# Left-hand sums of a joint feed-forward stage: built in PSUM beside the LayerNorm's transposes, with other banks and lanes around them

## The chip, the cores and the metric

The kernel runs on one core of a Trainium2 chip, in one launch. The metric is device time in microseconds. A core has TensorE (PE, matrix products into PSUM, with PEld for its weight loads), VectorE (DVE), ScalarE (ACT), GpSimd (POOL) and SyncE (SP), which here issues loads. PSUM has 8 banks of 128 partitions x 512 float32.

## The reference, cut to what matters

One decoder layer in float32, 1024 positions, width 1024. The change lies in its second part and just ahead of it.

```
mix = hybrid_mixer(x, ...)          # convolution group, attention group, output projection w_out
x   = layer_norm(ALPHA * x + mix, ln1_g, ln1_b)
h   = causal_depthwise_conv(x @ w_up, dw_w, dw_b)      # w_up: 1024 x 5632, conv width 3
g, u = jnp.split(h, 2, axis=-1)
ffn = (jax.nn.silu(g) * u) @ w_down                    # w_down: 2816 x 1024
x   = layer_norm(ALPHA * x + ffn, ln2_g, ln2_b)
```

In the mixer's convolution group a depthwise convolution of width 31 is followed by a LayerNorm over channels and a swish (`conv_norm` in the kernel).

## The kernel before, in words

**Precision.** Each float32 operand is split into a high part (a cast on ACT, L232, L280, L749) and a low part (the rest, by a subtraction). A product is three: high x high, high x low, low x high. So `mm3` (L266, L267, L269) issues 24 matmuls for 1024 inputs and `product` (L790, L791, L793) 12 for 512 inputs. Weights are split the same way into lanes `wh` (ACT) and `wl` (POOL, L234).

**Halves.** Positions are worked on in two halves of 512, H = 0 and 1, of four row blocks (t) each. After the mixer each half goes through the first LayerNorm (`ln1`), whose blocks are transposed on PE (L277), copied and split from PSUM (L280, L281) into `x1T[H]`: high and low parts of the channels' two halves, [128, 4, 512] each.

**Feed-forward.** D_FF is cut into 22 chunks of 128. The first six ("alone") are computed for each half separately: `up` (two `up_branch` products of 24 matmuls, convolution of width 3, silu, gate; L673 to L694) for two chunks, then `down` (L713 to L715, added to `acc` by L720). The other 16 ("joint") are computed for both halves at once with seven products instead of eight block products (a Strassen scheme): `joint_up` takes products of sums of weight blocks (`tsum`, L829, on POOL, lanes `ts`) with left-hand sides in `left`, some of which are sums of blocks of `x1T`. `left_sums` builds sums 1, 3 and 2 for k = 0 to 3 by DVE additions in SBUF lanes `u` (L743 for the first, L745 for further terms), and `keep` splits each into sums' areas (L749 on ACT, L750 on POOL). `last_sum` builds sum 4 the same way, just before `joint`. A chunk's products go in the order 1, 6, 7, 2, 5, 4, 3; the sums are used by products 6 (sum 2), 7 (sum 3), 5 (sum 1) and 3 (sum 4).

**Order.** `SCRIPT` is a string of letters, each of which takes one step of a generator: A attention of the second half, C its convolution, N its conv norm, o and O the output projections of the two halves, l and L the two first LayerNorms (four row blocks each), f the alone chunks of the first half (up, up, down, three times: f1 to f9), s the left-hand sums (four steps). What is left is drained at the end, then come `last_sum`, `joint`, and the second half's alone chunks. This is the order of emission. A planner in the build then places the instructions of each engine by its own model of costs and due times; the result is a fixed queue for each engine, with semaphores. Three kinds of work keep the emitted order: loads on SP (`load`), the large products on PE (`chain`), and the convolution's taps.

**PSUM.** `PT` names for each user a string of bank families, used in turn; `PS` says how many banks each family has: A 2, S 2, T 1, Y 1, C 2. The attention uses S for scores, T for transposes and Y for its output; the convolution and conv norm use C; the output projections A.

**SBUF.** Lanes are numbered pieces of 2 KB per partition. Tiles of one tag go through its lanes in turn, so a lane's next user waits for the last one's readers. `area(i)` is lanes 4i to 4i + 3 and `pair(i)` areas 2i and 2i + 1. The residual rows `acc` of the second half lie in lanes 64 to 71, loaded at the start of `second_out`; `pair(5)` is lanes 40 to 47, which hold the first half's attention output, later the gates of the first alone group (`gh`, `gl`), later sum 1. The rows g1 and b1 of the LayerNorm lie in lanes 94 to 97, where the lanes `u` also lie.

Of the kernel before, what the change touches and what calls it, by code (L numbers as in the profile page):

```python
# [10 lines left out]
F32 = mybir.dt.float32  # L11
F32R = mybir.dt.float32r
AF = mybir.ActivationFunctionType
ALU = mybir.AluOpType
# [20 lines left out]
GROUP = 2  # L35
ALONE = 6
SCRIPT = ('0hx00j0hxixxiiiacaaaaaaaaaaaaannnaaagaggqqgaaaqkqoAAAoAAAAAo'
          'ACAoAAllAANAAAANAlAlfNfAOOOfOffLLLLsffffsss')
SKEW = (1, 2, 5)
KOFF = (4, 5)  # L40
AHEAD = 1
# [1 line left out]
XM = (1, 1)  # L43
PT = {'x0': 'AT', 'x1': 'AS', 'glu0': 'AS', 'glu1': 'A', 'kv0': 'A', 'kv1': 'A', 'q0': 'A', 'q1': 'A', 'v0': 'T', 'v1': 'T',
      'joint': 'ATSACSYC',
      'tail': 'T', 'out0': 'A', 'out1': 'A', 'ln0': 'A', 'ln1': 'A', 'up0': 'AY', 'up1': 'AY', 'down0': 'SCY', 'down1': 'S'}
PS = {'A': 2, 'S': 2, 'T': 1, 'Y': 1, 'C': 2}
UNIT = 512
BASE = 384
# [7 lines left out]
    'oh': [16, 17, 18, 19, 20, 21], 'ol': [22, 23, 24, 25, 26, 27], 'or': [28, 30],  # L57
    'gh': [40, 41, 42, 43], 'gl': [44, 45, 46, 47],
}
LANES_NORM1 = {'nsum': [68, 69], 'nz': [70], 'nsq': [64, 65, 66, 67]}  # L60
LANES_OUT1 = {'bo': [32], 'oh': [48, 49, 50, 51, 52], 'ol': [53, 54, 55, 38, 39], 'or': [34, 36]}
LANES_FFN = {'gh': [D0 + i for i in range(28, 32)], 'gl': [D0 + i for i in range(24, 28)]}
LANES_JOINT = {'z': [D0 + i for i in (17, 18, 19, 36)],
               'ts': [D0 + i for i in (32, 33, 34)], 'u': [D0 + i for i in (20, 21, 22, 23)],
               'wl': [D0 + i for i in (12, 13, 14, 15, 16, 35)]}
FREE = [i for a in (0, 1, 2, 3, 5) for i in range(8 * a, 8 * a + 8)]
LANES_END = {'g2': [D0 + 32], 'b2': [D0 + 34], 'wl': [D0 + i for i in range(12, 17)], 'gh': FREE[0:6], 'gl': FREE[6:12], 'dh': FREE[12:24], 'dl': FREE[24:36]}

# [2 lines left out]
def hybrid_layer_kernel(  # L71
# [35 lines left out]
    def psk(key, shape=(P, 512)):  # L107
        tags = PT[key]
        k = ps_turn[key] = ps_turn.get(key, -1) + 1
        return psB(shape, tags[k % len(tags)])  # L110

    def f(ap):
        return ap.bitcast(F32)
# [156 lines left out]
        chain(m[0], m[-1])  # L270

    def transpose_split(src, xh, xl, t, key):
        for q in range(2):
            b = psk(key)
            for k in range(4):
                kt = q * 4 + k
                nc.tensor.transpose(out=b[:, k * P:(k + 1) * P], in_=src[:, kt * P:(kt + 1) * P], identity=ident)  # L277
            bv_ = b.rearrange("p (k t) -> p k t", t=P)
            hd = xh[q][:, :, t * P:(t + 1) * P]
            nc.scalar.copy(out=hd, in_=bv_)  # L280
            nc.vector.tensor_tensor(out=xl[q][:, :, t * P:(t + 1) * P], in0=bv_, in1=f(hd), op=ALU.subtract)  # L281

    def bcast_row(v, tag):
        t = sbt([P, D], tag)
# [39 lines left out]
    def pair(i):  # L324
        return area(2 * i), area(2 * i + 1)
# [330 lines left out]
    def ln1(H, g, b):  # L656
        (h0, l0), (h1, l1) = [pair(i) for i in ((2, 3) if H == 0 else (4, 6))]
        xh, xl = (h0, h1), (l0, l1)
        x1T[H] = (xh, xl)
        for t in range(TB):  # L660
            a = acc[H * TB + t]
            layer_norm_rows(a, g, b, H)
            transpose_split(a, xh, xl, t, "ln%d" % H)
            nc.scalar.mul(out=a, in_=a, mul=ALPHA)
            yield

    def up_branch(H, u):
# [68 lines left out]
    left = {}  # L736
    turns = [0]

    sums = {n: [[a[:, k, :] for k in range(4)] for a in pair(i)] for n, i in ((1, 5), (3, 0), (2, 1), (4, 2))}

    def add(o, *terms):
        (x0, s0), (x1, s1) = terms[0], terms[1]
        nc.vector.tensor_tensor(out=o, in0=x0, in1=x1, op=ALU.add if s1 > 0 else ALU.subtract)  # L743
        for x_, s_ in terms[2:]:
            nc.vector.tensor_tensor(out=o, in0=o, in1=x_, op=ALU.add if s_ > 0 else ALU.subtract)  # L745

    def keep(n, k, o):
        h, l = [x_[k] for x_ in sums[n]]
        nc.scalar.copy(out=h, in_=o)  # L749
        nc.gpsimd.tensor_tensor(out=l, in0=o, in1=f(h), op=ALU.subtract)  # L750

    def left_sums():
        a1h, a1l = x1T[1]
        a2h, a2l = x1T[0]

        o = {}
        for k in range(4):
            p1h, p1l, p2h, p2l = [[f(a[i][:, k, :]) for i in range(2)] for a in (a1h, a1l, a2h, a2l)]
            for n in (1, 3, 2):
                o[n] = sbt([P, HALF], "u")  # L760
                if n == 1:
                    add(o[n], (p2h[0], 1), (p2h[1], 1), (p2l[0], 1), (p2l[1], 1))
                elif n == 3:
                    add(o[n], (p1h[0], 1), (p2h[0], -1), (p1l[0], 1), (p2l[0], -1))
                else:
                    add(o[n], (o[1], 1), (p1h[0], -1), (p1l[0], -1))
                keep(n, k, o[n])
            yield

    def last_sum():  # L770
        a1h, a1l = x1T[1]
        a2h, a2l = x1T[0]
        for k in range(4):
            o = sbt([P, HALF], "u")
            s2h, s2l = [f(x_[k]) for x_ in sums[2]]
            add(o, (f(a1h[1][:, k, :]), 1), (s2h, -1), (f(a1l[1][:, k, :]), 1), (s2l, -1))
            keep(4, k, o)

        def ks(a):
            return [a[:, k, :] for k in range(4)]  # L780

        left.update({1: (ks(a1h[0]), ks(a1l[0])), 2: (ks(a1h[1]), ks(a1l[1])), 3: sums[4], 4: (ks(a2h[1]), ks(a2l[1])),
                     5: sums[1], 6: sums[2], 7: sums[3]})
# [211 lines left out]
    def second_norm():  # L995
# [4 lines left out]
             'c': conv(0), 'a': attn(0), 'n': conv_norm(0), 'g': glus(1), 'k': once(lambda: proj_kv(1)),  # L1000
             'q': proj_q(1), 'A': attn(1), 'o': out_proj(0), 'l': first_norm(), 'C': conv(1),
             'N': second_conv_norm(), 'f': ffn(0, alone), 'O': second_out(), 'L': second_norm(),
             's': left_sums()}
    drain(load_x(0))
    parameters()
    for k in SCRIPT:
# [64 lines left out]
```

## Time and profile before

| | |
|---|---|
| median of three runs | 1154.1 us (1151.25 to 1156.5) |
| the profiled execution's own time | 1154.67 us |
| its span, first to last instruction | 1152.9 us |
| mean granted TensorE clock | 0.958 |
| busy: PE, DVE, ACT, POOL | 1085.0, 796.6, 521.8, 627.5 us |
| second half's output projection | about 400 to 457 us |
| second half's LayerNorm, alone chunks f4 to f9, sums | about 450 to 559 us |
| joint stage, nothing else beside it | from about 563 us |

How to read it: a row of a group gives line, engine, operation, output tile <- input tiles, shapes, how many (x), then busy time in us and the mean ns of one, then the engine's idle time ahead of it and what ended it. A row of waits says who waited for whom: us in total, how often, the longest. A row of one source line gives the ns of the shortest, the median and the longest, and the first and last start. In the chain of waits a row gives start, length, engine, tile and line. The strip PEclk gives the granted clock in tenths over 40 equal slices. `psA`, `psT` and so on are banks of the families above; `x` is any area, `cy` the lanes that `u` shares with the convolution's outputs, `bo` the lanes of b1.

### The profile page before, as it was taken

The numbers are of one execution on the slowest core, as the hardware profiler recorded it, in microseconds if no ns is written. First come the engines' busy times: TensorE is split into PE (matmuls) and PEld (weight loads), VectorE is DVE, ScalarE is ACT, GpSimd is POOL, SyncE is SP. The second block draws the span as 40 slices with busy tenths as digits, with TensorE's granted clock in tenths as the row PEclk, the third lists the DMA queues.
The fourth block names the chain that finished last, engine by engine and source line by source line (L and its number), as shares of the span: only waits on it lengthen the run. The fifth ranks groups of instructions, "written<-read, shape, count | busy, mean of one in ns | idle before, by whom it ended". The sixth has DMA issues, their size and how long they took to land.

```text
span 1152.9 us, 14636 instructions
## 1 busy us (share of the span) xinstructions
PE 1085.0 (94%) x5257; PEld 907.7 (79%) x5257; DVE 796.6 (69%) x1406; ACT 521.8 (45%) x1031; POOL 627.5 (54%) x484
## 2 busy tenths in 40 slices
PE   7999999998898999894999999999999999999997
PEld 5877788888787799683778787887878787888875
DVE  2699556999994436889784747465665656559666
ACT  4536897673678322453342425152424242442530
POOL 4739644365451255867856556463637373735561
PEclk9999988999977899997999999999999999999999
DMA  5544213124101333221121212121202021133421
GB/s 177 165 100 120 74 26 98 52 85 144 38 1 54 102 99 94 76 71 37 37 73 37 74 37 74 37 65 32 69 19 89 22 73 37 56 109 110 128 92 73
DMA packets 115643, 85.21 MB, mean 74 GB/s; under 512 B 20355, under 2 KB 108018, under 8 KB 115570
## 3 DMA queue, kind: packets, MB, share of 16 engines
q1 hardware_dynamic: 112368, 78.92, 23.1%
q10 hardware_dynamic: 3201, 5.35, 1.3%
q8 instruction: 41, 0.67, 0.2%
q14 instruction: 33, 0.26, 0.1%
HBM read 80.05 MB, written 4.21 MB: 73 GB/s over the span
## 4 chain that ended last, share of the span: by engine, by line
PE 71%; DVE 18%; DMA 4%; ACT 4%; POOL 1%; issue 1%; SPq 0%; POOLq 0%; DVEq 0%; ACTq 0%
PE psA L266 4%; PE psA L267 4%; PE psA L269 4%; DVE psC L423 4%; DVE cy L745 3%; PE psC L793 2%; PE psS L509 2%; PE psC L790 2%; PE psC L791 2%; PE psS L713 2%; PE psS L714 2%; PE psS L715 2%; PE psS L790 2%; PE psS L791 2%; PE psS L793 2%; PE psA L790 2%
## 5 line engine op out<-in xcount | busy, mean ns | idle before, releaser
L234 POOL TENSOR_TENSOR wl<-raw,wh 128x512 fp32r<-128x512 f32 x196 | 267.3, 1375 | 187.4 <-ACT wh L232 80.8
L232 ACT CAST wh<-raw 128x512 fp32r<-128x512 f32 x196 | 118.9, 618 | 169.2 <-PE psA L267 26.8
L234 POOL TENSOR_TENSOR wl<-ts,wh 128x512 fp32r<-128x512 f32 x64 | 83.0, 1304 | 148.3 <-ACT wh L232 136.0
L423 DVE SCALAR_TENSOR_TENSOR psC<-hconv,const,psC 128x512 f32<-128x512 f32 x196 | 135.9, 745 | 0.0
L266 PE MATMUL psA<-x,wh 128*128 128x512 f32 x288 | 115.8, 402 | 3.1 <-ACT wh L232 2.0
L232 ACT CAST wh<-ts 128x512 fp32r<-128x512 f32 x64 | 39.4, 622 | 173.3 <-PE psC L715 31.0
L267 PE MATMUL psA<-x,wh 128*128 128x512 f32 x288 | 115.7, 402 | 0.0
L269 PE MATMUL psA<-x,wl 128*128 128x512 f32 x288 | 76.4, 400 | 0.0
L266 PEld LDWEIGHTS psA<-x,wh 128*128 128x128 f32 x288 | 55.2, 192 | 15.7 <-ACT wh L232 2.3
L267 PEld LDWEIGHTS psA<-x,wh 128*128 128x128 f32 x288 | 55.4, 192 | 11.9 <-issue 0.7
L269 PEld LDWEIGHTS psA<-x,wl 128*128 128x128 f32 x288 | 54.1, 191 | 12.7 <-issue 1.0
L291 POOL TENSOR_TENSOR tiny<-tiny,const 128x1 f32<-128x1 f32 (+1 forms) x28 | 26.5, 950 | 68.0 <-DVE tiny L290 68.0
L234 POOL TENSOR_TENSOR ol<-or,oh 128x512 fp32r<-128x512 f32 x32 | 40.5, 1292 | 32.5 <-ACT oh L232 32.5
L720 DVE TENSOR_TENSOR acc<-psS,acc 128x512 f32<-128x512 f32 x48 | 32.9, 687 | 24.5 <-PE psS L715 24.4
L790 PE MATMUL psS<-x,wh 128*128 128x512 f32 x112 | 43.7, 390 | 0.8 <-ACT wh L232 0.8
L790 PE MATMUL psA<-x,wh 128*128 128x512 f32 x112 | 44.2, 395 | 0.0
L791 PE MATMUL psA<-x,wh 128*128 128x512 f32 x112 | 44.0, 393 | 0.0
L791 PE MATMUL psS<-x,wh 128*128 128x512 f32 x112 | 43.6, 389 | 0.0
L790 PE MATMUL psC<-x,wh 128*128 128x512 f32 x112 | 43.6, 389 | 0.0
L791 PE MATMUL psC<-x,wh 128*128 128x512 f32 x112 | 43.6, 389 | 0.0
L413 POOL TENSOR_TENSOR cp<-cp,cp 128x512 f32<-128x512 f32 x28 | 36.1, 1289 | 13.3 <-ACT cp L409 13.3
L713 PE MATMUL psC<-wh,gh 128*128 128x512 f32 x80 | 32.5, 407 | 11.3 <-ACT gh L693 8.7
(331 smaller groups left out, 3237.5 us busy)
## 6 DMA issues: line engine op xcount, KB each, us to landing
raw<-in_w_up SPq DMA_DIRECT2D x56, 512.0 KB
raw<-in_w_down SPq DMA_DIRECT2D x28, 512.0 KB
raw<-in_w_in SPq DMA_DIRECT2D x20, 512.0 KB
raw<-in_x SPq DMA_DIRECT2D x8, 512.0 KB
raw<-in_w_in SPq DMA_DIRECT2D x16, 256.0 KB
acc<-in_x SPq DMA_DIRECT2D x8, 512.0 KB
or<-in_w_out SPq DMA_DIRECT2D x64, 64.0 KB
or<-in_w_out SPq DMA_DIRECT2D x8, 512.0 KB
```

The costliest lines, as they stand in the source:

```text
L232: nc.scalar.copy(out=h, in_=part)
L234: nc.gpsimd.tensor_tensor(out=l, in0=part, in1=f(h), op=ALU.subtract)
L266: m.append(nc.tensor.matmul(out=o, lhsT=wh[kt], rhs=xh[kt], start=kt == 0, stop=False))
L267: m.append(nc.tensor.matmul(out=o, lhsT=wh[kt], rhs=xl[kt], start=False, stop=False))
L269: m.append(nc.tensor.matmul(out=o, lhsT=wl[kt], rhs=xh[kt], start=False, stop=kt == KT - 1))
L413: nc.gpsimd.tensor_tensor(out=extra[c], in0=extra[c], in1=prod, op=ALU.add)
L423: tap(nc.vector.scalar_tensor_tensor(out=to, in0=src, scalar=cdw(k, c), in1=chains[c], op0=ALU.mult, op1=ALU.add))
L713: m.append(nc.tensor.matmul(out=o, lhsT=gh[:, tsl], rhs=wh, start=j == 0, stop=False))
L745: nc.vector.tensor_tensor(out=o, in0=o, in1=x_, op=ALU.add if s_ > 0 else ALU.subtract)
L790: m.append(nc.tensor.matmul(out=o, lhsT=wh[k], rhs=xh[k], start=k == 0, stop=False))
L791: m.append(nc.tensor.matmul(out=o, lhsT=wh[k], rhs=xl[k], start=False, stop=False))
L793: m.append(nc.tensor.matmul(out=o, lhsT=wl[k], rhs=xh[k], start=False, stop=k == 3))
```

## The change

- Left-hand sums. The first sum (of the first half's blocks only) becomes a generator of its own, `first_sums`: three additions in a PSUM bank of family T per k, then the split, its low part on DVE. Sums 3 and 2 and the unsplit sum 4 are built by `other_sums`, called in `ln1` for each row block of the second half: it goes on working in the two banks that the block's transposes filled (`transpose_split` now returns them), with the low parts on DVE as well. Sum 4 is parked in `last_f` (lanes 106 to 109, which `ts` uses later), and `last_sum` only splits it.
- Order: the four s steps move from the end to around the last O step, ahead of f4, f5 and the L steps.
- Banks: the second LayerNorm's transposes go from A to T and C in turn; the first half's alone chunks from A and Y to A (up) and from S, C and Y to S and Y (down); the first sums take T.
- Lanes: the second conv norm (`second_conv_norm`) takes its temporaries from lanes 40 and 42 to 47 instead of 64 to 70. The sixth `wl` lane is added in `last_sum` rather than at the first L step.

```
-SCRIPT = (...
-          'ACAoAAllAANAAAANAlAlfNfAOOOfOffLLLLsffffsss')
+          'ACAoAAllAANAAAANAlAlfNfAOOOfsOsssffLLLLffff')
-      ..., 'ln1': 'A', 'up0': 'AY', 'up1': 'AY', 'down0': 'SCY', 'down1': 'S'}
+      ..., 'ln1': 'TC', 'sum1': 'T', 'up0': 'A', 'up1': 'AY', 'down0': 'SY', 'down1': 'S'}
-LANES_NORM1 = {'nsum': [68, 69], 'nz': [70], 'nsq': [64, 65, 66, 67]}
+LANES_NORM1 = {'nsum': [44, 45], 'nz': [40], 'nsq': [42, 43, 46, 47]}
...
-            transpose_split(a, xh, xl, t, "ln%d" % H)
+            banks = transpose_split(a, xh, xl, t, "ln%d" % H)
             nc.scalar.mul(out=a, in_=a, mul=ALPHA)
+            if H == 1:
+                other_sums(t, *[b.rearrange("p (k t) -> p k t", t=P) for b in banks])
...
+    last_f = at((D0 + 32) * 4 * UNIT, [P, 4, HALF], F32, "lastf")
+    def part(x_, t):
+        return x_[:, :, t * P:(t + 1) * P]
+    def into(o, x0, x1, op):
+        nc.vector.tensor_tensor(out=o, in0=x0, in1=x1, op=op)
+    def split_to(h, l, o):
         nc.scalar.copy(out=h, in_=o)
-        nc.gpsimd.tensor_tensor(out=l, in0=o, in1=f(h), op=ALU.subtract)
+        into(l, o, f(h), ALU.subtract)
+    def first_sums():
+        (h0, h1), (l0, l1) = x1T[0]
+        for k in range(4):
+            o = psk("sum1")
+            into(o, f(h0[:, k, :]), f(h1[:, k, :]), ALU.add)
+            into(o, o, f(l0[:, k, :]), ALU.add)
+            into(o, o, f(l1[:, k, :]), ALU.add)
+            split_to(*[x_[k] for x_ in sums[1]], o)
+            yield
+    def other_sums(t, b0, b1):
+        (h0, h1), (l0, l1) = [[f(part(a, t)) for a in x_] for x_ in x1T[0]]
+        into(b0, b0, h0, ALU.subtract)
+        into(b0, b0, l0, ALU.subtract)
+        split_to(*[part(a, t) for a in pair(area_of[3])], b0)
+        into(b0, h1, b0, ALU.subtract)
+        into(b0, b0, l1, ALU.add)
+        s2h, s2l = [part(a, t) for a in pair(area_of[2])]
+        split_to(s2h, s2l, b0)
+        into(b1, b1, f(s2h), ALU.subtract)
+        into(part(last_f, t), b1, f(s2l), ALU.subtract)
     def last_sum():
...
-            add(o, (f(a1h[1][:, k, :]), 1), (s2h, -1), (f(a1l[1][:, k, :]), 1), (s2l, -1))
-            keep(4, k, o)
+            split_to(*[x_[k] for x_ in sums[4]], last_f[:, k, :])
+        lanes['wl'] = [D0 + i for i in (12, 13, 14, 15, 16, 35)]
```

More of the change, by code (lines that the diff above doesn't have):

```diff
@@ L45 @@
       'joint': 'ATSACSYC',
-      'tail': 'T', 'out0': 'A', 'out1': 'A', 'ln0': 'A', 'ln1': 'A', 'up0': 'AY', 'up1': 'AY', 'down0': 'SCY', 'down1': 'S'}
+      'tail': 'T', 'out0': 'A', 'out1': 'A', 'ln0': 'A', 'ln1': 'TC', 'sum1': 'T', 'up0': 'A', 'up1': 'AY', 'down0': 'SY', 'down1': 'S'}
 PS = {'A': 2, 'S': 2, 'T': 1, 'Y': 1, 'C': 2}
@@ L63 @@
 LANES_JOINT = {'z': [D0 + i for i in (17, 18, 19, 36)],
-               'ts': [D0 + i for i in (32, 33, 34)], 'u': [D0 + i for i in (20, 21, 22, 23)],
-               'wl': [D0 + i for i in (12, 13, 14, 15, 16, 35)]}
+               'ts': [D0 + i for i in (32, 33, 34)], 'u': [D0 + i for i in (20, 21, 22, 23)]}
 FREE = [i for a in (0, 1, 2, 3, 5) for i in range(8 * a, 8 * a + 8)]
@@ L272, in transpose_split @@
     def transpose_split(src, xh, xl, t, key):
+        banks = []
         for q in range(2):
             b = psk(key)
+            banks.append(b)
             for k in range(4):
@@ L281, in transpose_split @@
             nc.vector.tensor_tensor(out=xl[q][:, :, t * P:(t + 1) * P], in0=bv_, in1=f(hd), op=ALU.subtract)
+        return banks
     def bcast_row(v, tag):
@@ L737, in hybrid_layer_kernel @@
     turns = [0]
[L739 to L756, printed above, removed]
-        for k in range(4):
[L758 to L767, printed above, removed]
-            yield
+    area_of = {1: 5, 3: 0, 2: 1, 4: 2}
@@ new lines, in hybrid_layer_kernel @@
+    sums = {n: [[a[:, k, :] for k in range(4)] for a in pair(i)] for n, i in area_of.items()}
+    last_f = at((D0 + 32) * 4 * UNIT, [P, 4, HALF], F32, "lastf")
[4 more added lines that the diff above has]
+    def split_to(h, l, o):
+        nc.scalar.copy(out=h, in_=o)
+        into(l, o, f(h), ALU.subtract)
+    def first_sums():
+        (h0, h1), (l0, l1) = x1T[0]
+        for k in range(4):
+            o = psk("sum1")
[3 more added lines that the diff above has]
+            split_to(*[x_[k] for x_ in sums[1]], o)
+            yield
@@ L773, in last_sum @@
         for k in range(4):
-            o = sbt([P, HALF], "u")
-            s2h, s2l = [f(x_[k]) for x_ in sums[2]]
-            add(o, (f(a1h[1][:, k, :]), 1), (s2h, -1), (f(a1l[1][:, k, :]), 1), (s2l, -1))
-            keep(4, k, o)
+            split_to(*[x_[k] for x_ in sums[4]], last_f[:, k, :])
+        lanes['wl'] = [D0 + i for i in (12, 13, 14, 15, 16, 35)]
         def ks(a):
@@ L1002, in hybrid_layer_kernel @@
              'N': second_conv_norm(), 'f': ffn(0, alone), 'O': second_out(), 'L': second_norm(),
-             's': left_sums()}
+             's': first_sums()}
     drain(load_x(0))
```

## The prediction

> **What bounds the kernel now.** I read the page's head first, then the strips over the span, then the table of stretches, cut where the stages change.
>
> ```profile
> PE 1085.0 (94%) x5257; PEld 907.7 (79%) x5257; DVE 796.6 (69%) x1406; ACT 521.8 (45%) x1031; POOL 627.5 (54%) x484
> PEclk9999988999977899997999999999999999999999
> 347.00:400.00 53.00, 44.97 (x210) 40.21 (x209) 23.54 (x51) 31.65 (x65) 12.76 (x12) 0.77 0.27 84
> 400.00:457.00 57.00, 57.00 (x433) 55.03 (x432) 28.54 (x56) 13.72 (x23) 28.83 (x23) 1.00 0.33 98
> 457.00:480.00 23.00, 22.25 (x100) 18.04 (x98) 20.36 (x26) 7.68 (x12) 19.85 (x11) 1.00 0.23 69
> 480.00:501.00 21.00, 16.66 (x76) 13.37 (x76) 16.38 (x26) 12.12 (x21) 8.89 (x7) 0.84 0.17 50
> 501.00:523.00 22.00, 22.00 (x98) 18.02 (x96) 21.93 (x22) 9.49 (x16) 19.54 (x12) 1.00 0.28 83
> 523.00:563.00 40.00, 24.13 (x84) 18.65 (x84) 38.81 (x45) 13.34 (x23) 31.77 (x21) 0.79 0.07 21
> 563.00:1060.00 497.00, 488.77 (x2148) 402.43 (x2147) 313.02 (x524) 185.17 (x312) 270.00 (x211) 1.00 0.19 59
> ```
>
> In a stretch's row stand its length, the busy time of PE, PEld, DVE, ACT and POOL, then the granted clock. PE is busy for 488.77 of 497 us from 563 on, at full clock, and for all of 400 to 457: there only less PE work would help, and the change removes none. The loss lies in two places. From 457 to 563 PE is busy for 22.25 + 16.66 + 22.00 + 24.13 = 85.0 of 106 us, and the clock falls to 0.84 and 0.79. From 347 to 400 it idles for 8.0 us at a clock of 0.77.
>
> What ends last in 457 to 563 is said by the chain of waits there and by the waits of PE:
>
> ```profile
> 554.61 1.20 DVE cy L745 x2
> 555.81 1.20 DVE acc L720 x2
> 557.01 0.79 DVE cy L745
> 557.83 0.62 ACT x L749
> 558.45 0.53 ACT wh L232
> 559.02 0.50 PE psS L790
> 562.49 0.91 PE psS L793 x4
> PE psC L713 <- ACT gh L693: 8.7, 1, 8.7
> PE psT L790 <- ACT wh L232: 6.4, 1, 6.4
> PE psS L715 <- DVE gl L694: 2.2, 1, 2.2
> PE psY L713 <- DVE z L678: 2.1, 1, 2.1
> ```
>
> Before the third joint product (psS, 559.02) stands a row of DVE additions of the left-hand sums (L743, L745). They share DVE's queue with the gate of the last alone chunks, so that the down products (psC, L713) wait 8.7 us for a gate and the second joint product (psT) 6.4 us for its operands. So this stage is DVE's, and it is the one that the change rewrites.
>
> **The change part by part.** First, what DVE and POOL do for the sums now, and beside it the nearest instructions with a PSUM operand.
>
> ```profile
> L745 DVE TENSOR_TENSOR cy<-cy,x 128x512 f32<-128x512 f32 x28 | 30.9, 1119 | 0.1
> L743 DVE TENSOR_TENSOR cy<-x,x 128x512 f32<-128x512 f32 x12 | 16.2, 1353 | 0.0
> L743 DVE TENSOR_TENSOR cy<-cy,x 128x512 f32<-128x512 f32 x4 | 5.5, 1380 | 0.0
> L750 POOL TENSOR_TENSOR x<-cy,x 128x512 fp32r<-128x512 f32 x16 | 25.0, 1569 | 13.2 <-ACT x L749 13.2
> L745 DVE TENSOR_TENSOR cy<-cy,x x28: 674/1042/1779, 476.9 to 556.9; 128x512 f32<-128x512 f32 x28
> L838 DVE TENSOR_TENSOR psA<-psA,cy x16: 685/698/700, 566.2 to 1003.6; 128x512 f32<-128x512 f32 x16
> L281 DVE TENSOR_TENSOR x<-psA,x x8: 672/682/692, 481.2 to 502.9; 128x512 fp32r<-128x512 f32 x8
> L694 DVE TENSOR_TENSOR gl<-z,gh 128x512 fp32r<-128x512 f32 x4 | 6.0, 1492 | 0.1
> ```
>
> *Removed:* 44 DVE additions on SBUF, 30.9 + 16.2 + 5.5 = 52.6 us, and 16 subtractions on POOL, 25.0 us. The additions range from 674 to 1779 ns; the ones that read PSUM (L838 in place, L281) stay within 672 to 700.
>
> *Added on DVE:* per step of the first sum three additions and one subtraction (16 in all), per row block of the second LayerNorm eight instructions (32), and four subtractions of the last sum. The 48 with a PSUM operand I cost at 0.68 (L281): 32.6 us. The four on SBUF cost between 0.67 and 1.78 each, by L745's ends: 2.7 to 7.1, taken as 4.5 by its mean. Sum 37 us for 52.6, and POOL's 25 us fall to nothing. The 16 casts on ACT stay 16 (row 557.83: 0.62), 12 of them now from PSUM.
>
> *Moved:* the first sums stand ahead of the second LayerNorm in the order of emission; they need only the first half. They write lanes 40 to 47, which the first alone group's gates also use, so they wait for that group's down products, the last at about 445. DVE is busy for 28.54 of 57 us in 400 to 457, which covers about half of their 16 x 0.68 = 10.9 us. A split that stands too early in ACT's or DVE's queue would hold up the evictions of the output projection behind it, two banks deep; the planner knows the lanes, so I put that at 0. The other sums run per row block and needn't wait for all four blocks nor for the g1 and b1 rows, whose lanes the old sums shared.
>
> *What PE can gain at most from 457 to 563.* The stage holds 8 x 24 alone-chunk matmuls, 96 of down products, 36 of the first three joint products, and 32 transposes.
>
> ```profile
> 495.50 0.87 PE psA L277 x8
> 489.36 0.43 PE psY L714
> L277 PE MATMUL psA<-const,acc 128*128 128x128 f32 x32 | 5.0, 292 | 0.0
> L280 ACT CAST x<-psA x8: 575/584/592, 474.0 to 500.2; 128x512 fp32r<-128x512 f32 x8
> ```
>
> At full clock four matmuls take 0.91 (row 562.49), so 324 take 73.7; 32 transposes at 0.87 for eight, 3.5; together 77.2 of 106 us. Of the 28.8 lost, 21.0 are idle and 85.0 - 77.2 = 7.8 a slow clock (a matmul takes 0.43 at 489.36): 0.37 us for each idle one.
>
> *What stays idle.* The f6 and f9 down products still wait for a gate: 2.2 + 2.1 before f6, of which I keep 3.0, since the other sums now stand in DVE's queue at that place; of f9's 8.7 I keep 3.5 (bounds: 0, if the first joint product, 12 matmuls or 2.7 us, and others fill it, and 8.7 as now). Of the 6.4 for the second product's operands 1.0 stays, because the sums for it are finished block by block; bounds 0 and 6.4. The down products of the alone chunks now alternate between S and Y, where Y has a single bank: a Y unit must be evicted within the 1.4 us of the S unit beside it (6 matmuls), by an addition of 0.68 queued behind at most two others of 0.68. That leaves 0 to 0.7 for each of the 8 Y units of f6 and f9; taken 2.0, bounds 0 and 5.6. Idle 9.5, slow clock 0.37 x 9.5 = 3.5: 13.0 of the 28.8 stay, the gain is 15.8.
>
> *Can DVE do it in that time?* From 457 to 563 it is busy for 20.36 + 16.38 + 21.93 + 38.81 = 97.5. Less 52.6, plus 32 x 0.68 + 4.5 and 6 of the first sums, is 77.2; L694, at 1492 ns instead of the 0.68 it takes undisturbed, may give back 3 more. Before the second joint product must stand all but the last sum (4.5) and f9's eight additions (5.4): some 67 us, against 77.2 of PE work. DVE fits, narrowly.
>
> *The T bank.* Each row block now holds a T bank through four transposes, three casts and seven DVE instructions: 0.44 + 3 x 0.58 + 7 x 0.68 = 6.9 us, some 9 with hand-overs, four blocks 36. The norms are ready from about 460, so the chain ends near 496, or 516 if each hand-over waits for one more DVE instruction. The second joint product comes later than that. Nothing on the path.
>
> *Other lanes for the second conv norm.* The next rows show what its old lanes (64 to 70) cost.
>
> ```profile
> SPq L132 <- PE psC L478: 56.5, 2, 56.0
> 289.24 0.58 SPq L132 DMA_DIRECT2D bo<-in_b_out  x1
> 368.70 2.13 SPq L132 DMA_DIRECT2D acc<-in_x  x4
> 312.75 1.27 POOL L428 TENSOR_TENSOR cy<-cy,cp 128x512 f32<-128x512 f32 x1 [1.15 <-DVE cy L423]
> L266 PE MATMUL psA<-x,wh x16: 389/389/393, 346.7 to 391.1; 128*128 128x512 f32 x16
> L266 PE MATMUL psY<-x,wh x16: 387/396/628, 381.2 to 397.5; 128*128 128x512 f32 x16
> ```
>
> The residual rows for the second half (acc, 64 to 71) wait on the load queue for the norm's last squares, 56 us, and all w_out loads behind them. With the new lanes they need only the convolution's end (314.0). What this uncovers is small: the output projection starts at 400 behind four alone-chunk products, which PE owes anyway. The gain depends on these moving into the 8.0 idle us of 347 to 400. The first chunk's second product (psY) starts at 381.2, 34 us after its first (psA, 346.7), while the attention uses Y; it now takes a bank of its own family, A, and may go earlier. One product is 24 x 0.2275 = 5.5 us. Bounds: 0 (the attention's chain simply shifts) and 8.0 plus 3 of clock; I take 4 + 1 of clock = 5.
>
> *A and wl.* Up products on A alone have two banks where three served; a bank must be free one product (5.5) after it is filled, and its eviction takes a cast and three DVE instructions, under 3. Cost 0 while DVE isn't over 2 us late; without that cover, 1 us per product. The weights' lower parts have five lanes instead of six until the last sum: 0, since 24 matmuls use four.
>
> *Sum:* -15.8 - 5.0 = -20.8 against the profiled execution's own 1154.67 us: 1133.9. The median of the runs, 1154.1, stands 0.6 lower, so 1133.3.
>
> **A rule weighed.** The row first: PE idled 2.2 and 2.1 us before 488.6 (L694 and L678 above), and at 489.36 a matmul took 0.43 instead of 0.23. The Trainium skill, "TensorE: Matmul & The Clock Gate", section "HAM oscillation — how this bites in real kernels", says that PE should have no idle gaps over some 3.4 us, or it falls back to the slow clock. By that rule the gaps that I leave, of 3.5 us at most in parts, would cost no clock. The trace disagrees in part: two shorter gaps close together were enough. My slow-clock term goes by the trace.
>
> **The rivals.**
> 1. *Full clock.* If the gaps that remain are too short and too far apart to slow PE, the 3.5 of clock go too, and with f6's wait halved 1.5 more: 1128. For it: 400 to 457 and 501 to 523 hold 1.00 throughout. Against: the 0.84 of 480 to 501, with gaps of about 2.
> 2. *DVE still ends last.* The LayerNorm's rows now carry 5.4 us more each, and the gates queue behind them. If DVE is busy nine tenths of the time its 67 us end at 457 + 74 = 531, and if f9's gate comes only then, its 10.9 us of down products (48 matmuls) and the second and third product (5.4) follow one another: the third ends at 531 + 4 + 10.9 + 5.4 = 551 instead of 563. With a further 4 of slow clock 8 remain, and nothing from the lanes: 1146. For it: DVE is 97 per cent busy in 523 to 563. Against: the gate of f9 has no call to wait for sums that are due later.
> 3. *It does nothing:* the sums go faster, but the order written by the planner leaves PE waiting for weights in the same places. 1154. Against: waits for DMA are missing among the long ones of this stage.
> 4. *Slower: the alone chunks' banks.* With S and Y alone, 16 down units of f6 and f9 wait for evictions behind sums in DVE's static order. Each must lose 1.3 us to eat the 20.8, and more than 1.65 to end 0.5% slower; at three DVE instructions late (2.0) it is 32 us: 1165. For it: DVE's load. Against: L720 evicts in 0.68, and every third or second instruction there is independent of PE.
>
> **How the numbers follow.** The forecast (1130 to 1143) has 0.52, full clock (below 1130) 0.14, DVE last (1143 to 1151) 0.17, nothing 0.10, slower 0.07. 0.5% or 5.8 us is about what a measurement of this kernel can tell. Faster takes the first two and most of the third, 0.80; within 0.5% is 0.13; slower 0.07. The range leaves out some 0.06 below 1121 (both stages without any idle would end at 1154 - 28.8 - 8 = 1117) and 0.13 above 1150.
>
> **What would show it.** Right: third joint product ending near 545 instead of 563 in the profile; no additions over 1 us among the sums; PE idle under 12 us where it was 21; acc loads issued near 315 and PE idle under 5 in the stretch before the output projection. Wrong: PE waits on evictions (L720) of psY or psS; a T bank released after 516; the gate's wait of f9 still over 6; any idle in the long joint stage, which should stay at 98% busy.

## The result and the profile after

| | before | after |
|---|---|---|
| median (lowest to highest, 4 runs each) | 1155.3 us (1151.25 to 1156.86) | 1140.87 us (1134.79 to 1141.53) |
| profiled execution, own time and span | 1154.67 and 1152.9 us | 1140.95 and 1139.2 us |

The ratio is 0.9877, with a 95% interval of 0.9849 to 0.9904: the change is faster by 1.2%. The forecast was 1133.3 us, in a range of 1121 to 1150. In the new kernel lines have other numbers: the down products are L717 to L719, their eviction L724, the joint products L797 to L800, every addition and subtraction of the sums L751 and every cast of them L754, the up products L265 to L268.

From the head and the strips of the page after:

```profile
span 1139.2 us, 14637 instructions
PE 1084.8 (95%) x5257; PEld 903.9 (79%) x5257; DVE 776.6 (68%) x1414; ACT 521.3 (46%) x1031; POOL 599.1 (53%) x468
PEclk9999988999968899999999999999999999999998
```

DVE has 20 us less to do and POOL 28; PE's work is what it was. The table of stretches after, cut at the same events as before (columns: length, then PE, PEld, DVE, ACT, POOL, granted clock, DMA share, GB/s):

```profile
300.00:347.00 47.00, 38.74 (x206) 34.03 (x205) 44.69 (x99) 25.88 (x70) 23.66 (x15) 0.75 0.17 56
347.00:398.40 51.40, 46.69 (x233) 38.66 (x231) 24.12 (x55) 35.68 (x76) 6.01 (x6) 0.87 0.03 11
398.40:458.20 59.80, 59.78 (x454) 57.65 (x455) 33.78 (x66) 16.73 (x31) 34.90 (x29) 1.00 0.39 116
458.20:550.24 92.04, 82.74 (x357) 65.85 (x357) 76.69 (x118) 41.39 (x69) 53.96 (x38) 0.96 0.20 58
550.24:1047.00 496.76, 488.99 (x2149) 402.61 (x2148) 312.12 (x525) 184.56 (x311) 268.37 (x209) 1.00 0.19 59
```

The stage between the output projection and the fourth joint product lasts 92.04 us; before, its counterpart began at 456.8 and lasted to 563.2, 106.4 us. PE idles for 92.04 - 82.74 = 9.3 us in it, where it was 21. The long joint stage is as it was, 496.76 for 497.00. So nearly all that was won lies in this one stage, 14.4 us, and nothing was won ahead of it: its start moved from 456.8 to 458.2. The chain that ended last, where the third joint product (psS) goes before the fourth (psA, from 550.24):

```profile
546.48 1.20 PE psT L800 x4
...
549.50 0.91 PE psS L800 x4
```

Before, the rows ahead of the third product were DVE's additions, and it ended at 562.49 + 0.91 = 563.40. Now PE follows PE, and it ends at 550.41. What PE still waits for, from 458 to 551 (who waits, for whom; us in total, times, longest):

```profile
PE psA L265 <- DVE z L682: 3.5, 2, 2.9
PE psS L717 <- ACT gh L697: 2.8, 1, 2.8
PE psT L800 <- POOL wl L233: 0.9, 1, 0.9
PE psT L797 <- ACT wh L231: 0.9, 1, 0.9
PE psA L268 <- POOL wl L233: 0.6, 1, 0.6
PE psA L265 <- ACT wh L231: 0.3, 1, 0.3
PE psS L719 <- DVE gl L698: 0.2, 1, 0.2
```

The gate's wait of f9 went from 8.7 to 2.8 us and the second product's operands from 6.4 to 0.9 + 0.9. New is an up product that waits for a bank of family A (z, L682, is the last read of one), 3.5 us. The sums on DVE, grouped with their shapes:

```profile
L751 DVE TENSOR_TENSOR psT<-psT,x 128x512 f32<-128x512 f32 x20 | 13.8, 689 | 0.1
L751 DVE TENSOR_TENSOR x<-psT,x 128x512 fp32r<-128x512 f32 x12 | 8.2, 684 | 2.9 <-ACT x L754 2.7
L751 DVE TENSOR_TENSOR psT<-x,x 128x512 f32<-128x512 f32 x4 | 4.1, 1026 | 0.0
L751 DVE TENSOR_TENSOR psC<-psC,x 128x512 f32<-128x512 f32 x4 | 2.8, 688 | 0.0
L751 DVE TENSOR_TENSOR psT<-x,psT 128x512 f32<-128x512 f32 x4 | 2.7, 686 | 0.0
L751 DVE TENSOR_TENSOR lastf<-psC,x 128x512 f32<-128x512 f32 x4 | 2.7, 682 | 0.0
L751 DVE TENSOR_TENSOR x<-lastf,x 128x512 fp32r<-128x512 f32 x4 | 2.5, 681 | 0.0
L751 DVE TENSOR_TENSOR psT<-x,x x4: 689/692/2031, 407.5 to 465.6; 128x512 f32<-128x512 f32 x4
```

They sum to 36.8 us where the old additions took 52.6. Two groups have both inputs in SBUF: the first step of the first sums (psT<-x,x) and the last subtractions (x<-lastf,x). Only the former has a mean over 1 us, and the last row shows that a single instruction of 2031 ns makes it so; the others take some 690.

Where the forecast's 5 us from the lanes went is told by the loads of the second half's residual rows (acc), by the scaled additions that follow them on DVE (one source line in each kernel: ns of shortest, median, longest, then first and last start), and by the last transposes of the first half's LayerNorm on PE (start, length). First after, its loads ahead (the last transposes, x4, are the end of a block's eight); then before, with its row of the table of stretches for 300 to 347:

```profile
313.11 1.76 SPq L131 DMA_DIRECT2D acc<-in_x  x4
L627 DVE SCALAR_TENSOR_TENSOR acc<-acc,bo x4: 1207/1212/1891, 316.8 to 330.2; 128x1024 f32<-128x1024 f32 x4
354.32 0.66 PE L278 MATMUL psA<-const,acc 128*128 128x128 f32 x4 [0.50 <-DVE x L282]
```

```profile
300.00:347.00 47.00, 41.93 (x251) 37.11 (x251) 45.42 (x106) 31.80 (x88) 23.39 (x15) 0.82 0.00 1
L625 DVE SCALAR_TENSOR_TENSOR acc<-acc,bo x4: 1212/1224/1226, 372.1 to 378.1; 128x1024 f32<-128x1024 f32 x4
342.71 1.13 PE L277 MATMUL psA<-const,acc 128*128 128x128 f32 x8
```

The loads leave at 313.11 instead of 368.70, as forecast. But with them come four additions of 1.2 to 1.9 us on DVE, at 316.8 to 330.2 instead of 372.1 to 378.1. There DVE is busy for 44.69 of 47 us (45.42 before), and the first half's LayerNorm is in the same queue: its last transposes end at 354.32 + 0.66 = 354.98 instead of 342.71 + 1.13 = 343.84, 11.1 us later.

### The profile page after: what moved, and what is told of

It reads as the page before. It is cut to its first block, busy times and chain, and to the rows that moved or that the text cites. A ratio compares the mean times of both kernels' runs of the same rounds, so it can differ in the third digit from the quotient of the medians.

```text
span 1139.2 us, 14637 instructions
## 1 busy us (share of the span) xinstructions
PE 1084.8 (95%) x5257; PEld 903.9 (79%) x5257; DVE 776.6 (68%) x1414; ACT 521.3 (46%) x1031; POOL 599.1 (53%) x468
## 4 chain that ended last, share of the span: by engine, by line
PE 45%; DVE 5%; ACT 1%; DMA 0%; POOL 0%; issue 0%; POOLq 0%; ACTq 0%
PE psC L800 2%; PE psC L798 2%; PE psC L797 2%; PE psS L800 2%; PE psS L797 2%; PE psS L798 2%; PE psA L800 2%; PE psA L798 2%; PE psA L797 2%; PE psS L717 2%; PE psS L718 2%; PE psS L719 2%; PE psA L717 1%; PE psC L717 1%; PE psA L718 1%; PE psA L719 1%
## 5 line engine op out<-in xcount | busy, mean ns | idle before, releaser
L233 POOL TENSOR_TENSOR wl<-raw,wh 128x512 fp32r<-128x512 f32 x196 | 263.0, 1354 | 223.4 <-PE psA L268 86.3
L265 PE MATMUL psA<-x,wh 128*128 128x512 f32 x336 | 138.2, 411 | 7.9 <-DVE z L682 3.5
L266 PE MATMUL psA<-x,wh 128*128 128x512 f32 x336 | 137.4, 409 | 0.0
L268 PE MATMUL psA<-x,wl 128*128 128x512 f32 x336 | 90.6, 404 | 0.6 <-POOL wl L233 0.6
L265 PEld LDWEIGHTS psA<-x,wh 128*128 128x128 f32 x336 | 66.1, 197 | 24.0 <-issue 4.4
L266 PEld LDWEIGHTS psA<-x,wh 128*128 128x128 f32 x336 | 66.0, 197 | 14.6 <-issue 0.7
L268 PEld LDWEIGHTS psA<-x,wl 128*128 128x128 f32 x336 | 63.9, 193 | 15.8 <-issue 1.2
L724 DVE TENSOR_TENSOR acc<-psS,acc 128x512 f32<-128x512 f32 x52 | 35.6, 687 | 26.9 <-PE psS L719 26.9
L797 PE MATMUL psS<-x,wh 128*128 128x512 f32 x112 | 43.6, 389 | 0.0
L797 PE MATMUL psA<-x,wh 128*128 128x512 f32 x112 | 43.6, 389 | 0.0
L798 PE MATMUL psA<-x,wh 128*128 128x512 f32 x112 | 43.6, 389 | 0.0
L797 PE MATMUL psC<-x,wh 128*128 128x512 f32 x112 | 43.6, 389 | 0.0
L836 POOL TENSOR_TENSOR ts<-raw,ts 128x512 f32<-128x512 f32 x32 | 41.6, 1299 | 1.2
```

What stands on the lines that cost most here:

```text
L233: nc.gpsimd.tensor_tensor(out=l, in0=part, in1=f(h), op=ALU.subtract)
L265: m.append(nc.tensor.matmul(out=o, lhsT=wh[kt], rhs=xh[kt], start=kt == 0, stop=False))
L266: m.append(nc.tensor.matmul(out=o, lhsT=wh[kt], rhs=xl[kt], start=False, stop=False))
L268: m.append(nc.tensor.matmul(out=o, lhsT=wl[kt], rhs=xh[kt], start=False, stop=kt == KT - 1))
L797: m.append(nc.tensor.matmul(out=o, lhsT=wh[k], rhs=xh[k], start=k == 0, stop=False))
L798: m.append(nc.tensor.matmul(out=o, lhsT=wh[k], rhs=xl[k], start=False, stop=False))
```

## The experiments

Five theories are told apart. D: the new lanes cost time, since the early loads bring DVE work into a stretch in which DVE is full. S: the sums in PSUM alone carry the gain. I: sums and banks need each other; the banks alone only bring the output projection's end forward. C: alone products that share family C with the sums wait there, and that eats the gain. K: a sum's addition in SBUF is slow because of POOL beside it.

All the runs that follow, in one table. "First alone" is the start of the first alone product (L265 or L266), "O ends" the start of the output projection's last matmul, "stage" the time from there to the first matmul of the fourth joint product, all from the one profiled execution's timeline; the ratio is that of the timed runs to the kernel before, run on the same chip. The experiments ran in groups on three chips, on which the kernel before took medians of 1153.7, 1154.8 and 1153.6 us, and 1155.3 beside the kernel after. So kernels are compared by their ratios; a hundredth is 11.5 us.

| kernel | sums | up0, down0 | lanes | median us | ratio (95%) | first alone | O ends | stage |
|---|---|---|---|---|---|---|---|---|
| before | SBUF | AY, SCY | old | | 1 | 346.7 | 456.7 | 106.6 |
| after | PSUM | A, SY | new | 1140.87 | 0.9877 (0.9849 to 0.9904) | 356.4 | 458.0 | 92.2 |
| lanes_old | PSUM | A, SY | old | 1131.56 | 0.9811 (0.9782 to 0.9841) | 345.2 | 447.4 | 91.1 |
| late_scale | PSUM | A, SY | new | 1134.48 | 0.9837 (0.9807 to 0.9867) | 352.5 | 450.5 | 91.8 |
| lanes_only | SBUF | AY, SCY | new | 1161.44 | 1.0054 (1.0033 to 1.0076) | 356.0 | 464.2 | 106.6 |
| up_ay | PSUM | AY, SY | new | 1151.86 | 0.9971 (0.995 to 0.9992) | 355.9 | 463.2 | 96.4 |
| sums_only | PSUM | AY, SCY | old | 1153.01 | 0.9995 (0.9976 to 1.0015) | 347.6 | 458.3 | 107.6 |
| banks_only | SBUF | A, SY | old | 1151.58 | 0.9973 (0.9955 to 0.9991) | 346.0 | 450.6 | 108.6 |
| lo_scy | PSUM | A, SCY | old | 1139.35 | 0.9863 (0.9842 to 0.9885) | 347.5 | 448.6 | 99.9 |
| up_ac | PSUM | AC, SY | old | 1134.13 | 0.9833 (0.9806 to 0.986) | 341.8 | 446.0 | 96.2 |
| keep_dve | SBUF, low parts on DVE | AY, SCY | old | 1152.33 | 0.999 (0.9973 to 1.0007) | 346.2 | 456.1 | 104.9 |
| order_old | PSUM, s at the end | A, SY | old | 1134.74 | 0.9828 (0.9796 to 0.986) | 345.1 | 450.0 | 93.2 |
| l_first | PSUM, L earlier | A, SY | old | 1132.39 | 0.9813 (0.9784 to 0.9842) | 344.9 | 448.5 | 92.0 |

**The old lanes (lanes_old).** The kernel after, with the conv norm's lanes put back:

```diff
-LANES_NORM1 = {'nsum': [44, 45], 'nz': [40], 'nsq': [42, 43, 46, 47]}
+LANES_NORM1 = {'nsum': [68, 69], 'nz': [70], 'nsq': [64, 65, 66, 67]}
```

> The changed kernel with the second conv norm's temporaries back in lanes 64 to 70. Theory D (displaced work): with the new lanes the residual rows land at about 315, and their four scale-and-add instructions on DVE (1.2 us each) stand ahead of the first half's LayerNorm in a stretch in which DVE is busy all the time; that put the first alone product from 346.7 to 356.4 and ate the 5 us that I had forecast. With the old lanes they run after 370 again: the first product starts near 347 and the kernel is 4 to 7 us faster than the changed one (about 1134 to 1137). Rival P: it is the alone products, now on A alone, that stand ahead of the attention on PE and make it end at 400 instead of 381; then the lanes change nothing: within 2 us of the changed kernel.

1131.56 us: by the ratios 0.66% or some 7.6 us faster than the kernel after, with intervals that don't meet. It beats both kernels and has the lowest ratio here, though the intervals of late_scale, up_ac, order_old and l_first overlap with its own. The up products' first lines (L265), first after, then lanes_old:

```profile
L265 PE MATMUL psA<-x,wh x32: 389/389/796, 356.4 to 393.0; 128*128 128x512 f32 x32
```

```profile
L265 PE MATMUL psA<-x,wh x32: 389/389/628, 345.2 to 375.2; 128*128 128x512 f32 x32
347.00:400.00 53.00, 48.37 (x282) 42.91 (x281) 29.53 (x61) 30.96 (x65) 13.64 (x12) 0.90 0.27 83
447.60:538.40 90.80, 79.63 (x357) 63.38 (x356) 76.67 (x117) 41.42 (x69) 53.83 (x38) 1.00 0.20 59
```

With the old lanes the first four alone products start 11 to 19 us earlier, and the output projection ends 10.6 us earlier. The stage behind it hardly differs (91.1 and 92.2). So the lanes cost time ahead of O, as D says, and more than it was given.

**The new lanes alone (lanes_only)**, the same line changed the other way in the kernel before.

> The kernel before with the second conv norm's new lanes alone. Theory D: the four scale-and-add instructions go ahead of the first LayerNorm on DVE, the first alone product starts 6 to 10 us later; but the second one waits for the attention's Y bank until 381 here, so part of it is hidden: 0 to 6 us slower than before. Rival E: the loads that land 55 us earlier let the output projection start earlier: 3 us or more faster.

1161.44 us, slower by 0.54% or 6.2 us, at the upper end of what was foreseen, and O ends 7.5 us later with the same stage of 106.6 behind it. The lanes cost time with the old sums and banks too.

**Early loads, late additions (late_scale).** The kernel after, with the four scaled additions held back behind the first alone product's first tap:

```diff
-                nc.vector.scalar_tensor_tensor(out=a, in0=a, scalar=ALPHA, in1=bo, ...)
+                i = nc.vector.scalar_tensor_tensor(out=a, in0=a, scalar=ALPHA, in1=bo, ...)
+                if H == 1:
+                    tc.add_manual_dep(i.ins, first_tap[0].ins.name, order, ...)
...
+        if first_tap[0] is None:
+            first_tap[0] = i      # the first tap, L683
```

> The changed kernel, new lanes kept, loads early, but the four scale-and-add instructions of the residual rows are tied behind the first alone product's first convolution instruction on DVE. Theory D: as with the old lanes, 4 to 7 us faster than the changed kernel, and no slower than with the old lanes (loads land earlier). If instead the early loads themselves or the aliased lanes cost the time: no gain, while the old lanes gain.

In DVE's timeline the four now stand together, behind that tap:

```profile
363.79 0.74 DVE L683 SCALAR_TENSOR_TENSOR z<-psA,const,z 128x511 f32<-128x511 f32 x1
364.45 5.70 DVE L628 SCALAR_TENSOR_TENSOR acc<-acc,bo 128x1024 f32<-128x1024 f32 x4
```

1134.48 us, with the loads as early as they were. By the ratios 0.40% of the 0.66% comes back, but the interval overlaps with that of the kernel after as well as with that of lanes_old, so the times alone don't show it. The profiles point the same way: O ends at 450.5, so that 7.5 of its delay of 10.6 us are gone. So the additions' place on DVE is, by the profile, most of what the lanes cost. It isn't all: the first alone product starts at 352.5, still 7.3 us later than in lanes_old, and what holds it there stays open.

**The sums alone (sums_only).** The kernel after with the old banks of the alone chunks and the old lanes:

```diff
-      ..., 'up0': 'A', 'up1': 'AY', 'down0': 'SY', 'down1': 'S'}
+      ..., 'up0': 'AY', 'up1': 'AY', 'down0': 'SCY', 'down1': 'S'}
```

> The changed kernel with both side changes undone: old lanes for the second conv norm, A and Y for up, S, C and Y for down. What is left is the sums in the transposing banks, T and C for the second LayerNorm's transposes, and the order. Theory S: the sums alone carry the whole gain: 13 to 15 us faster than before (1139 to 1142), since the third joint product ended 13.0 us earlier and O ended 1.2 us later in the changed kernel. Rival B: the parted banks carry a good part, and this gains under 8 us.

1153.01 us, no gain at all, though the 52.6 us of additions and POOL's 25 us are gone as in the kernel after. S falls. PE's waits from 450 to 575:

```profile
PE psC L717 <- DVE lastf L751: 8.0, 1, 8.0
PE psY L717 <- ACT gh L697: 4.8, 1, 4.8
PE psT L278 <- DVE x L751: 3.2, 1, 3.2
```

A down product of an alone chunk waits 8.0 us for its bank of family C, which holds a row block's transposes until the last subtraction (lastf) has read it. This is the longest wait of the stage, and the transposes wait 3.2 us for the T bank. A good part of the time that DVE saves is so lost to banks; that these waits are the whole loss is not shown, since waits for gates remain as well.

**The banks alone (banks_only).** The same strings set to A and SY in the kernel before.

> The kernel before with the banks alone changed: up on A, down on S and Y; the sums, the order and the lanes as before. With the sums alone the kernel is as slow as before, with sums and banks (old lanes) 22 us faster. Theory I (the two need each other): the banks bring the output projection's end from 457 to about 448, as with the old lanes, and nothing behind it, where the additions in SBUF still end last: 8 to 11 us faster than before, about 1143 to 1146. Rival B: the banks are the gain, and this comes within 4 us of 1131.6. Rival N: without the sums they give nothing, 1151 to 1155.

1151.58 us, 0.3% or 3.1 us faster where I foresaw 8 to 11: a miss, and the time is within what the rival N had given. O does end 6.1 us earlier, as I says, but the stage behind it is 2.0 longer, and the last stretch of the program, behind the joint stage, took 96.9 us for 92.9 in the execution that was profiled, at a granted clock of 0.96 for 0.98. The stage's waits are still for gates, with the slow additions in SBUF in the same queue:

```profile
PE psS L713 <- ACT gh L693: 14.8, 4, 8.2
```

So the sums alone give a ratio of 0.9995, the banks alone 0.9973, both together 0.9811: each needs the other, which is the half of I that holds.

**One bank string at a time (up_ay, lo_scy, up_ac).** up_ay is the kernel after with `'up0': 'AY'`; lo_scy and up_ac are lanes_old with `'down0': 'SCY'` and `'up0': 'AC'`.

> The changed kernel with the first half's up products on A and Y in turn, as before. Theory D: no gain, 0 to 4 us slower than the changed kernel, since the second product then waits for the attention's Y bank (381) while the late LayerNorm stays. Rival P: the attention is no longer held up, and the kernel is 4 to 6 us faster than the changed one.

> The version with the old lanes (1131.6), with the first half's down products back on S, C and Y. Theory C: the C banks are held by the other sums until their last instruction (in the run with the sums alone PE waited 8.0 us for psC behind the parked fourth sum), so down waits: 7 to 12 us slower than 1131.6, with PE waiting on psC behind line lastf. Rival Y: it was only Y, shared by up and down, that cost; with up on A nothing is lost, within 3 us of 1131.6, or a little faster for having five banks.

> The version with the old lanes (1131.6), with the first half's up products on A and C in turn: a third and fourth bank, but C is held by the other sums. Theory C (shared C banks wait for the parked fourth sum): 4 to 12 us slower than 1131.6, with PE's up products of f7 and f8 waiting for psC behind line lastf. Rival: the wait for a bank at f7 (2.9 us) goes and nothing comes for it: 1 to 4 us faster.

up_ay is 0.94% or 11 us slower than the kernel after, where 0 to 4 us were foreseen: a miss. Its second alone product starts at 387.1, since the attention's last product on Y starts at 383.6 and is still to be read, and O ends 5.2 us later; the rest is lost in the stage, in waits for gates, from 450 to 575:

```profile
PE psS L717 <- ACT gh L697: 10.3, 2, 5.7
```

Y is a bank in which no sum stands. So the dearest of the three strings is one of which C says nothing, and why its gates come late is not shown.

lo_scy is 0.52% or some 6 us slower than lanes_old, a little less than the 7 to 12 of C, and most of the profile's loss lies in the stage (99.9 for 91.1; O ends 1.2 later). But no wait on lastf shows in its longest waits, from 445 to 570:

```profile
PE psA L265 <- ACT wh L231: 3.1, 1, 3.1
PE psT L278 <- DVE x L751: 3.0, 1, 3.0
PE psA L265 <- DVE z L682: 2.9, 1, 2.9
448.70:548.50 99.80, 86.96 (x359) 68.89 (x358) 79.00 (x116) 41.38 (x69) 53.54 (x37) 0.91 0.18 53
```

PE waits for the T bank that the sums hold, and for a weight cast. The last row is the stage: against lanes_old's row above, PE idles 12.8 us for 11.2, and its work takes 87.0 for 79.6 at a granted clock of 0.91 for 1.00. So in this one execution most of the loss is the clock, not a wait for a bank. The planner has put the instructions in another order, and how the C bank leads to this is not shown. up_ac is 0.22% or some 2.5 us slower than lanes_old, below the 4 to 12 of C, and their intervals overlap. C is thus borne out in part by sums_only's wait and lo_scy's time, and not by up_ac.

**The low parts on DVE (keep_dve).** The kernel before, with L750's 16 subtractions moved from POOL:

```diff
-        nc.gpsimd.tensor_tensor(out=l, in0=o, in1=f(h), op=ALU.subtract)
+        nc.vector.tensor_tensor(out=l, in0=o, in1=f(h), op=ALU.subtract)
```

> The kernel before with the low parts of the sums on DVE instead of POOL (16 subtractions). Theory K: POOL stretches DVE's additions on SBUF; with its 25 us of subtractions gone the 44 additions fall from 52.6 to 38 to 45 us, DVE gains 11 us of subtractions, and the time stays within 5 us. Rival: the additions stay over 50 us, since POOL's weight splits alone keep them stretched; then the kernel is 5 to 11 us slower.

```profile
L745 DVE TENSOR_TENSOR cy<-cy,x 128x512 f32<-128x512 f32 x28 | 25.4, 920 | 0.0
L750 DVE TENSOR_TENSOR x<-cy,x 128x512 fp32r<-128x512 f32 x16 | 15.0, 941 | 0.0
L743 DVE TENSOR_TENSOR cy<-x,x 128x512 f32<-128x512 f32 x12 | 12.5, 1045 | 0.0
L743 DVE TENSOR_TENSOR cy<-cy,x 128x512 f32<-128x512 f32 x4 | 4.3, 1085 | 0.0
```

The same 44 additions take 42.2 us instead of 52.6, with nothing changed in them but the work beside them: K holds. The trace of the kernel before says the same without any edit: 11 of its 44 additions ran with no POOL instruction beside them, and each took 674 to 680 ns; the 33 others took 675 to 1779. The 16 subtractions cost DVE 15.0, so it has 4.6 us more in all, and the time is the same (0.999).

**The order (order_old, l_first).** lanes_old with the old order of s, f and L, and with two L steps ahead of the last f's:

```diff
-          'ACAoAAllAANAAAANAlAlfNfAOOOfsOsssffLLLLffff')
+          'ACAoAAllAANAAAANAlAlfNfAOOOfOffLLLLsffffsss')     # order_old
+          'ACAoAAllAANAAAANAlAlfNfAOOOfsOsssLfLfLLffff')     # l_first
```

> The version with the old lanes (1131.6), with the four steps of the first sums back at the end of the order of emission (after the LayerNorm's four row blocks). Theory F: the earlier place matters, because the first sums then use DVE before the LayerNorm's blocks come and share the T bank with them otherwise: 3 to 8 us slower than 1131.6. Rival: the planner puts instructions by due time, so the place in the script changes little: within 2 us.

> The version with the old lanes (1131.6), with the LayerNorm's row blocks and the alone chunks f4, f5 taken in turn (LfLfLL instead of ffLLLL). In 1131.6 PE still waits 2.9 us for a bank behind DVE's convolution, 2.7 and 1.1 for gates and 2.6 for the second product's operands. Theory G: with blocks begun earlier the T chain ends earlier and these shrink: 1 to 4 us faster. Rival: the sums then go ahead of f5's gate on DVE and f6 waits longer: 1 to 5 us slower.

Neither can be told from lanes_old: 0.17% and 0.02% more, with overlapping intervals. So neither the 3 to 8 us foreseen for the order nor the 1 to 4 foreseen for the earlier L steps came, and that the new order is worth anything isn't shown.

## Why the prediction was right, and where its terms were off

The median is 7.6 us above the forecast, inside the range. The forecast's sum had two terms. The first and larger, -15.8 in the stage, came out as -14.4, and it is why the forecast held. The third joint product ended at 550.4, where the sign for "right" had put some 545. The second, -5.0 ahead of it, came out as +1.4. The second one is the step that failed. Within the first, several parts were off and offset one another; that their sums came out so near is luck, as the paragraphs below say.

*Other lanes for the second conv norm, with bank A.* The prediction saw the loads move to 315 and wrote "What this uncovers is small", with bounds of 0 and a gain. It looked at what waits for the loads on SP and PE, and not at what the loads release: four instructions on DVE, some 5.5 us, into a stretch in which a row of the table of stretches (45.42 of 47 us) would have shown DVE to be full. Holding these back behind the first tap (late_scale) moves O's end from 458.0 to 450.5. Under the term lie two parts of opposite sign. The lanes end O 7.5 us later on the kernel before (lanes_only) and 10.6 later on the rest of the change (after against lanes_old). The banks end it 6.1 earlier (banks_only). The part that it did name, the second product on A instead of Y, is real: without the lanes that product starts at 350.7 instead of 381.2, and the term would have been -9.3 (447.4 for 456.7). The step's sign for "right", PE idle under 5 us ahead of O, is barely met after (51.40 - 46.69 = 4.7) and says nothing: the idle time had moved into 300 to 347, where PE is busy for 38.74 us instead of 41.93.

*The alone chunks' banks.* The forecast priced A alone and S with Y alone as costs, at 0 and 2.0 us, and nowhere as a gain in the stage. They are the condition of the whole gain: without them 0.9995. Most of this can't be laid to the sums' own families, since putting the up products back on Y costs more (up_ay, 0.94%) than giving C back to the down products (lo_scy, 0.52%), each against the kernel it was made from. The term itself was wrong in its parts as well: no wait for S or Y is among the rows after, and the bank A wait that was put at 0 took 3.5 us. That cover failed where DVE was late with the reads of A, the point that the text had named.

*DVE's sums.* Forecast 37 us, measured 36.8, by two errors that offset. The four that had been set apart at 4.5 us, the last sum's subtractions, took 2.5; the other 48, at 0.68 each or 32.6 in all, took 34.3. Most of this excess is one addition of the first sums: it reads both inputs from SBUF and took 2031 ns. The sign "no additions over 1 us" held for all but this one.

*What stays idle.* Forecast 9.5 us, measured 9.3, but of other parts, so that the agreement is luck:

| term | forecast | after |
|---|---|---|
| gate of f6 | 3.0 | 0.2 |
| gate of f9 | 3.5 | 2.8 |
| second product's operands | 1.0 | 1.8 |
| S and Y evictions | 2.0 | not among the waits |
| bank A | 0 | 3.5 |
| weights of the alone products | 0 | 0.9 |

The first row's 3.0 rested on two waits of the kernel before, 2.2 and 2.1 us. The second of them (psY, L713, behind z, L678) wasn't one for a gate: L678 is the up products' last read of their bank, so PE waited there for Y, which up has left.

*The slow clock.* Forecast 3.5 us over a stage of 77.2 at full clock. lanes_old shows the same 357 matmuls at a granted clock of 1.00, in 79.63 us: the floor was 2.4 too low, and after pays 82.74 - 79.63 = 3.1 for the clock. That is more than the 1.4 by which the first term fell short; idle time and clock gave a little of it back. Why the floor was too low stays open.

*The T bank.* The forecast had the chain of sums end between 496 and 516. The tile in which sum 4 is parked tells of its last step:

```profile
L751 DVE TENSOR_TENSOR lastf<-psC,x x4: 677/680/692, 494.9 to 532.7; 128x512 f32<-128x512 f32 x4
```

It ended at 533, and the last read of a T bank began at 530.9 (x<-psT,x, L751): the sign for "wrong" that named 516 was there. It cost the second product nothing that shows: that waited 0.9 for a cast of weights and 0.9 for their low part. "Nothing on the path" holds in the kernel after. In sums_only and lo_scy, where the down products use C, the transposes wait 3.2 and 3.0 for the T bank, and in sums_only a down product waits 8.0 for C.

*The rivals.* "Full clock" did not come about in the kernel after (0.96 in the stage); lanes_old has it, with gaps that are no shorter. "It does nothing" is what the sums alone would have done, though not by waits for weights. "DVE still ends last" is not what happened: in the chain PE follows PE. The rival that was slower, the alone chunks' banks, had it the wrong way round.

## What to carry to other kernels

When a wait is taken from a load, list what the loaded data releases, on every engine, and look in the table of stretches whether the engine is free there: an early load may cost nothing, and the work that follows it may. Arithmetic moved into PSUM banks is paid for in bank time; ask who else takes turns in that family, and in the other families that their users share, before counting the engine time saved. Price the parts of a change in pairs: here two that give nothing and 0.3% alone give 1.9% together, and a third part took more than a third of it away.

## What the runs showed of the hardware

**The clock after a gap.** Both kernels have the same two gaps of PE in this stage. After, by PE's timeline, with stretches about the first gap:

```profile
487.86 0.56 PE L265 MATMUL psA<-x,wh 128*128 128x512 f32 x1 [2.87 <-DVE z L682]
531.75 0.50 PE L717 MATMUL psS<-wh,gh 128*128 128x512 f32 x1 [2.76 <-ACT gh L697]
484.69:488.10 3.41, 0.54 (x3) 0.27 (x2) 3.41 (x6) 0.29 (x1) 1.70 (x1) 1.00 0.54 154
488.10:491.51 3.41, 3.41 (x9) 2.67 (x9) 2.59 (x6) 1.48 (x3) 0.00 (x0) 0.50 0.00 0
```

And lanes_old:

```profile
477.21 0.47 PE L265 MATMUL psA<-x,wh 128*128 128x512 f32 x1 [2.90 <-DVE z L682]
520.81 0.50 PE L717 MATMUL psS<-wh,gh 128*128 128x512 f32 x1 [2.71 <-ACT gh L697]
471.90:475.32 3.42, 2.16 (x9) 1.24 (x7) 3.42 (x6) 0.86 (x2) 3.42 (x2) 1.00 0.38 115
475.32:478.73 3.41, 1.52 (x7) 1.31 (x8) 2.59 (x6) 1.57 (x3) 0.41 (x1) 1.00 0.40 118
```

After gaps of 2.87 and 2.76 us the granted clock was 0.50 for one stretch of 3.41 us each (488.10 to 491.51, and 532.47 to 535.88); after gaps of 2.90 and 2.71 it stayed at 1.00 (the row 447.60:538.40). So the length of a gap doesn't decide here. Nor need two gaps lie close together, as in the prediction's reading of the kernel before: 44 us lie between those of after.

What decides is where a gap falls. In each of the thirteen traces all changes of the granted clock from 300 to 600 us lie on one grid with steps of 3.413 us, to within 1 ns, and the grid lies elsewhere in each trace. After's first gap fills most of one step, in which PE is busy for 0.54 us. Lanes_old's first gap lies across an edge of its grid, at 475.32 (reckoned on from its last change of clock, at 386.57), and leaves PE busy for 2.16 and 1.52 us in the two steps. From 400 to 600 us the thirteen traces hold 715 steps at full clock. Half clock followed 32 of them, in all of which PE idled for 1.77 us or more; in the 683 others PE idled for 1.89 us at most. So about half a step of idle time is enough. The two gaps of 2.2 and 2.1 us in the kernel before fit: of the step from 482.84 to 486.25 PE was idle for 1.98 us.

The Trainium skill, "TensorE: Matmul & The Clock Gate", section "What's actually happening", describes a free-running activity window that doesn't start with the work. The traces agree, with the grid of 3.413 us. So whether a gap of 2 to 3 us costs clock depends on where the grid happens to lie. With one trace for each kernel, that it moves between executions of one kernel is not shown.

**Two SBUF inputs beside POOL.** keep_dve's 42.2 us for 52.6, and the additions of before with and without a POOL instruction beside them (the latter all at 674 to 680 ns), agree with the Trainium skill, "SBUF — State Buffer", section "Who interferes with whom": a DVE instruction with two SBUF inputs contends with a GpSimd instruction that reads SBUF, and one with a single SBUF input does not. Here the groups with one input in PSUM took 682 to 689 ns on average, and those with both in SBUF 920 to 1380, but for the four last subtractions at 681 ns; from 536 to 539, where these stand, POOL was busy for 0.09 of 3.00 us. Not every addition beside POOL is stretched: some of the 33 took 675 to 679 ns too.
